# Gate products ahead of the convolution's layer norm, and five of 31 convolution taps summed on GpSimd

## The chip, the cores and the metric

The kernel runs on one core of one Trainium2 chip. The time is device microseconds (us) of one execution; a verdict compares runs of two kernels on the same chip. One execution is also recorded by the hardware profiler, and the trace comes from that one. Engines are named as the profile does: PE (TensorE matmuls), DVE (VectorE), ACT (ScalarE), POOL (GpSimd), SP (SyncE, which issues most weight transfers).

## The reference, cut to what matters

Three transformer blocks run over one sequence of 512 tokens of 1,024 channels, in float32. The change lies in the first. That block normalises its input and projects it to queries, keys and values of a sparse attention, to the two inputs of a convolution branch, and to two sets of gates. Attention and convolution branch are each multiplied by a gate, added, projected, and added to the input; a feed-forward part follows. The convolution branch is

```python
def conformer_conv(u_a, u_b, conv_w, conv_b, ln_g, ln_b, w_o, b_o):
    z = u_a * jax.nn.sigmoid(u_b)
    zp = jnp.pad(z, ((0, 0), (CONV_WIDTH - 1, 0), (0, 0)))      # 31 taps
    z = lax.conv_general_dilated(zp, conv_w, ...,
                                 feature_group_count=CONV_DIM) + conv_b
    mu = jnp.mean(z, axis=-1, keepdims=True)
    var = jnp.mean(jnp.square(z - mu), axis=-1, keepdims=True)
    zn = (z - mu) * lax.rsqrt(var + EPS) * ln_g + ln_b
    return jax.nn.silu(zn) @ w_o + b_o
```

It is a depthwise convolution: each channel has its own 31 weights, and each output is the sum of 31 shifted and scaled copies of `z`. Its output is normalised over the channels, so the mean needs all 1,024 of them. The gate of the branch is a product of the block's normalised input with a 1,024 x 1,024 matrix; it doesn't depend on the convolution.

## The kernel before

Activations lie with channels on the 128 partitions and the 512 tokens along them, so 1,024 channels are eight chunks, and the stack `X[:, c]` holds one chunk each. A float32 product is made of three matmuls of fp32r halves: `gemm` (L168 to L173) takes, for each of eight input chunks, `wh` by the high part, `wh` by the low part and `wl` by the high part, 24 matmuls of 128x512 for one output chunk. A weight unit of 512 KB (`wunit`) is fetched by an SP transfer into one of two `wst` buffers, ACT copies it in two pieces to `wh` (L155), POOL subtracts to get the remainder `wl` (L156), with four buffers of each kind. So every unit of weights needs SP, ACT and POOL before PE can use it, and PE has to be done before the buffers come free.

Block 1 runs in stages. In the projections, gates and inputs of the convolution are made chunk by chunk: `conv_gate` and `conv_in` (L650 to L664) leave a padded `z` of one chunk, and `conv_taps` (L666) sums its taps into a PSUM tile `y`: ACT writes the first tap with the bias (L671), DVE adds thirty (L673), ACT copies the sum to `X[:, c]` (L674). Between them come the keys, values and queries: rotary products on POOL (L706), stacks of split keys and queries (`stacks`, L1690; POOL at L1698 and L1705), and the compressed keys (L754 to L756). Attention then runs over four groups and four blocks of queries: scores, row maximum on DVE (L937), exponential on ACT, scaling by 1/sum partly on POOL (L949), transposes and products (L956 to L967). Three of the eight chunks of the convolution and the attention gates are interleaved with it.

After attention (L1006 on) the branch's layer norm collects its sums with `norm.feed(k)`: a first column sum of chunks 0 and 1 (L292, a matmul with ones into `pm` at L198, ACT at L295) gives a rough mean `c`, each chunk is centred by it (L306) and its square summed (L277), and two more column sums give mean and variance (L321 to L326); Ln and Exp on ACT (L216, L217) and three DVE operations (to L224) give `r`. Then eight gate products `w1_gc` run, DVE scales each by the block's norm (L680) and ACT takes the tanh (L1015). Last, each chunk is scaled by `r` (L336), passed through the activation (L1024), split into `zn` (L193, L194) and multiplied by `w1_co`; L1031 and L1032 multiply by the gate and add attention.

The order on each engine is fixed when the program is built: a scheduler goes through the program as written and by priorities. Weight units have a raised priority. The convolution's taps have one lowered by 3,000, so that they are put where DVE has nothing more urgent; wherever they land, each engine executes its own list strictly in order.

Of the kernel before, what the change touches and what calls it, by code (L numbers as in the profile page):

```python
# [13 lines left out]
AF = mybir.ActivationFunctionType  # L14
# [3 lines left out]
ADD, SUB, MUL, MAX, MIN = ALU.add, ALU.subtract, ALU.mult, ALU.max, ALU.min  # L18

P = 128  # L20
T = 512
NT = 8
# [16 lines left out]
MTB = 1  # L39
PS2 = dict(g=2, m=2, iv=2, rc=1, o=1)  # L40
HP = (30,60,0)
FIN = ("DDDDDDDD", "DDPDDPDD")
FLO = 1000
SQP = (2,4)
# [546 lines left out]
def block1(K, X, entry):  # L591

    K.hp = HP[0]
    nc, I, tc = K.nc, K.I, K.tc
# [23 lines left out]
    for k in range(NT):  # L618
# [4 lines left out]
        s = acc[k] if k < 2 else K.tmp()  # L623
# [33 lines left out]
    def conv_in(c):  # L657
        pa = K.gemm(K.gps(), gx, K.wunit(I["w1_ua"][c]))
        a = K.tmp()
        nc.vector.scalar_tensor_tensor(a, pa, 0.5, R, op0=MUL, op1=MUL)  # L660
        z = pz.tile([P, 30 + T], F32, tag="z", name=K.nm("z"))
        nc.gpsimd.memset(z[:, :30], 0.0)
        nc.vector.scalar_tensor_tensor(z[:, 30:], zb.pop(c), 1.0, a, op0=ADD, op1=MUL)
        conv_taps(c, z)  # L664

    def conv_taps(c, z):  # L666
        w = lambda k: K.v("conv_w", c * 31 + k)
        with tc.high_priority(offset=-LOW):

            y = K.ps("y")  # L670
            nc.scalar.activation(y, z[:, 0:T], AF.Identity, scale=w(0), bias=K.v("conv_b", c))  # L671
            for k in range(30, 0, -1):
                nc.vector.scalar_tensor_tensor(y, z[:, k:k + T], w(k), y, op0=MUL, op1=ADD)  # L673
            nc.scalar.activation(X[:, c], y, AF.Copy)  # L674

    def proj(w, scale=None, out=None):
        ps = K.gemm(K.gps(), gx, w if isinstance(w, list) else K.wunit(w))
        s = K.tmp() if out is None else out
        if scale is None:
            nc.vector.tensor_tensor(s, ps, R, MUL)  # L680
        else:
            nc.vector.scalar_tensor_tensor(s, ps, scale, R, op0=MUL, op1=MUL)
        return s

    sw = []
    for i in range(2):
        t = pA.tile([P, T], F32, name=f"swp{i}")
# [141 lines left out]
    for i in range(2):  # L829
        t = pA.tile([P, 640], F32R, name=f"KCz{i}")  # L830
# [4 lines left out]
    for i in range(2):  # L835
        t = pA.tile([P, 2, 4, P], F32R, name=f"PCz{i}")
# [170 lines left out]
    sC = ExitStack()  # L1007
    norm = Norm(0, K, X, 1e-6, sC)
    pC = sC.enter_context(tc.tile_pool(name="b1d", reuse_waits="tile", bufs=16))
    for k in range(NT):  # L1010
        norm.feed(k)
    sgc = []
    for m in range(NT):
        sgc.append(pC.tile([P, T], F32, tag="gc", bufs=8, name=K.nm("gc")))
        nc.scalar.activation(sgc[m], proj(I["w1_gc"][m]), AF.Tanh, scale=0.5)  # L1015
    zn = []
    alloc = lambda tag: (lambda: pC.tile([P, T], F32R, tag=tag, name=K.nm(tag)))
    for k in range(NT):
        norm.apply(k)
        y = X[:, k]  # L1020
        nc.scalar.activation(y, y, AF.Identity, scale=K.v("conv_norm_g", k), bias=K.v("conv_norm_b", k))
        t = norm.tmp()
# [31 lines left out]
    for qi, nk in enumerate(FFN_CUTS):  # L1054
        hid = []
        for m in range(at, at + nk):
# [3 lines left out]
            t = K.tmp()  # L1060
# [11 lines left out]
        for m in range(NT):  # L1072
            ps = K.gemm(K.gps(), hid, down(m))
            if tail:
                y = K.tmp()
# [86 lines left out]
def block2(K, X, entry, es):  # L1162
    K.hp = HP[1]
    nc, I, tc = K.nc, K.I, K.tc
# [544 lines left out]
def block3(K, X, rms, out, norm, es):  # L1709
    K.hp = HP[2]  # L1710
    nc, I, tc = K.nc, K.I, K.tc
# [305 lines left out]
    def after(m, sl):  # L2017
# [4 lines left out]
        with tc.high_priority(offset=0 if sl.stop == T else -FLO):  # L2022
            for k in range(NT):
                x = X[:, k, sl]
                if FIN[sl.stop == T][k] == "D":
                    nc.vector.scalar_tensor_tensor(x, x, K.v("g_final", k), r6.R[:, sl], op0=MUL, op1=MUL)
# [8 lines left out]
def program(tc, I, out, first=1, last=3):  # L2035
    with ExitStack() as es:
# [7 lines left out]
        if first == 1:  # L2044
            block1(K, X, entry)
        else:
            tc.nc.sync.dma_start(X, I["x_in"].rearrange("(c p) t -> p c t", p=P))
            K.psum(g=5, m=3)
# [36 lines left out]
```

## Time and profile before

| | us |
|---|---|
| median of 3 runs | 2908.86 |
| lowest and highest | 2906.74, 2912.71 |
| the profiled execution | 2904.16 |
| its span in the trace | 2902.4 |
| TensorE's mean granted clock in it | 0.972 of full speed |

In the profile an engine's busy time leaves out its waits and its register and semaphore instructions. A wait is put down to what released it last. In the timeline a row with x4 stands for four instructions that followed without a gap, and the bracket gives the idle time in front of it and its releaser. "PEclk" is the granted clock, with 1.00 for 2.4 GHz and 0.50 for 1.2.

### The profile page before, as it was taken

To read this page: it belongs to the slowest core of one execution; us is meant where nothing else is said; L and a number is where in the kernel's file an instruction comes from. 1 tells how busy PE (TensorE), PEld (TensorE's weight loads), DVE (VectorE), ACT (ScalarE), POOL (GpSimd) and SP (SyncE) were. 2 spreads that over 40 slices of the span, in tenths; PEclk is the share of its full clock that TensorE was granted. 3 is DMA by queue.
4 is the path that set the end of the run, shared out by engine and by line. 5 is a ranking of instruction groups with operands and counts; after the bars stand their busy time and mean duration, and the time that the engine had idled before them with its cause. 6 is when DMAs were issued, how large, how long until landed. Compare 5 with 4: busy or idle time off the path is not lost.

```text
span 2902.4 us, 34153 instructions
## 1 busy us (share of the span) xinstructions
PE 2676.3 (92%) x12206; PEld 2120.0 (73%) x12206; DVE 1780.9 (61%) x2825; ACT 1283.2 (44%) x2317; POOL 1306.6 (45%) x1023
## 2 busy tenths in 40 slices
PE   7899999699999988988889999999988889999997
PEld 5677776478888856766676788877766678788885
DVE  7889899965243596776774821126877765422246
ACT  4357875533222354444443533332556652322234
POOL 6554432554444454333332644454544344444443
PEclk9999999799999999999999999999999899999999
DMA  3321111232322222222222222232222122222223
GB/s 115 114 86 54 54 38 37 77 105 91 98 95 94 95 67 96 70 78 73 70 70 68 67 101 95 95 116 88 94 89 75 49 80 87 92 98 95 95 95 102
DMA packets 79193, 243.32 MB, mean 84 GB/s; under 512 B 11312, under 2 KB 15320, under 8 KB 79024
## 3 DMA queue, kind: packets, MB, share of 16 engines
q1 hardware_dynamic: 79024, 241.15, 25.3%
q8 instruction: 96, 1.57, 0.2%
q14 instruction: 73, 0.60, 0.1%
HBM read 230.96 MB, written 4.52 MB: 81 GB/s over the span
## 4 chain that ended last, share of the span: by engine, by line
PE 63%; DVE 23%; ACT 6%; DMA 3%; issue 3%; POOL 2%; SPq 0%; DVEq 0%; ACTq 0%; POOLq 0%
PE pg L172 18%; PE pg L173 18%; PE pg L171 18%; DMA B<-diag 2%; DVE p L1894 1%; DVE py L673 1%; DVE X L336 1%; DVE QK L1310 1%; PE ppt L956 1%; POOL wl L156 1%; DMA diag<-dg 1%; DVE ln L277 1%; DVE Zt L1416 1%; PE ps L934 1%; DVE Z L1417 1%
## 5 line engine op out<-in xcount | busy, mean ns | idle before, releaser
L156 POOL TENSOR_TENSOR wl<-wst,wh 128x512 fp32r<-128x512 f32 (+1 forms) x808 | 1099.9, 1367 | 1367.1 <-ACT wh L155 1285.7
L155 ACT ACTIVATE wh<-wst 128x512 fp32r<-128x512 f32 (+1 forms) x808 | 500.8, 627 | 1102.1 <-PE pg L172 918.1
L171 PE MATMUL pg<-op,wh 128*128 128x512 f32 (+1 forms) x2008 | 812.7, 405 | 38.9 <-ACT wh L155 19.5
L172 PE MATMUL pg<-op,wh 128*128 128x512 f32 (+1 forms) x2008 | 808.6, 403 | 2.6 <-DVE op L191 2.4
L173 PE MATMUL pg<-op,wl 128*128 128x512 f32 (+1 forms) x2008 | 807.2, 402 | 3.9 <-POOL wl L156 3.9
L171 PEld LDWEIGHTS pg<-op,wh 128*128 128x128 f32 (+1 forms) x2008 | 386.7, 193 | 120.9 <-ACT wh L155 20.1
L173 PEld LDWEIGHTS pg<-op,wl 128*128 128x128 f32 (+1 forms) x2008 | 386.2, 192 | 83.6 <-POOL wl L156 6.7
L172 PEld LDWEIGHTS pg<-op,wh 128*128 128x128 f32 (+1 forms) x2008 | 387.3, 193 | 82.2 <-DVE op L191 5.8
L171 PE MATMUL pg<-hid,wh 128*128 128x512 f32 x688 | 272.2, 396 | 0.9 <-DVE hid L190 0.9
L173 PE MATMUL pg<-hid,wl 128*128 128x512 f32 x688 | 272.1, 396 | 0.0
L172 PE MATMUL pg<-hid,wh 128*128 128x512 f32 x688 | 271.8, 395 | 0.2 <-DVE hid L191 0.2
L673 DVE SCALAR_TENSOR_TENSOR py<-z,vec,py 128x512 f32<-128x512 f32 x240 | 180.2, 751 | 10.9 <-ACT py L671 6.2
L1120 DVE TENSOR_TENSOR X<-X,pg 128x512 f32<-128x512 f32 x56 | 38.5, 688 | 222.1 <-PE pg L173 222.1
L171 PEld LDWEIGHTS pg<-hid,wh 128*128 128x128 f32 x688 | 129.2, 188 | 32.9 <-DVE hid L190 1.3
L172 PEld LDWEIGHTS pg<-hid,wh 128*128 128x128 f32 x688 | 129.2, 188 | 31.9 <-DVE hid L191 0.5
L173 PEld LDWEIGHTS pg<-hid,wl 128*128 128x128 f32 x688 | 129.2, 188 | 31.3 <-issue 0.2
L190 DVE CAST hid<-t 128x512 fp32r<-128x512 f32 x86 | 53.0, 616 | 145.7 <-ACT t L1097 145.0
L1111 DVE SCALAR_TENSOR_TENSOR t<-pg,R 128x512 f32<-128x512 f32 x32 | 22.1, 691 | 84.0 <-PE pg L173 83.9
L938 ACT ACTIVATE P<-ps,s 128x128 f32<-128x128 f32 (+3 forms) x128 | 66.4, 523 | 11.6 <-DVE s L937 9.5
L191 DVE TENSOR_TENSOR hid<-t,hid 128x512 fp32r<-128x512 f32 x86 | 63.6, 740 | 3.0
L937 DVE TENSOR_REDUCE s<-ps 128x1 f32<-128x128 f32 (+3 forms) x128 | 60.1, 483 | 8.1 <-PE ps L936 6.6
L960 DVE TENSOR_TENSOR PTl<-ppt,PTh 128x512 fp32r<-128x512 f32 x80 | 53.4, 684 | 4.7 <-ACT PTh L959 3.9
(523 smaller groups left out, 4344.3 us busy)
## 6 DMA issues: line engine op xcount, KB each, us to landing
wst<-in_w_f_dram SPq DMA_DIRECT2D x64, 512.0 KB
wst<-in_w_up_dram SPq DMA_DIRECT2D x32, 512.0 KB
wst<-in_w_down_dram SPq DMA_DIRECT2D x32, 512.0 KB
wst<-in_w_ga_dram SPq DMA_DIRECT2D x24, 512.0 KB
wst<-in_w_fg_dram SPq DMA_DIRECT2D x22, 512.0 KB
wst<-in_w_fu_dram SPq DMA_DIRECT2D x22, 512.0 KB
wst<-in_w_q_dram SPq DMA_DIRECT2D x16, 512.0 KB
wst<-in_w_out_dram SPq DMA_DIRECT2D x16, 512.0 KB
```

The source lines that it names most:

```text
L155: nc.scalar.activation(h, st, AF.Copy)
L156: nc.gpsimd.tensor_tensor(l, st, h, SUB)
L171: self.nc.tensor.matmul(ps, lhsT=wh, rhs=h[:, sl], start=first and k == 0, stop=False)
L172: self.nc.tensor.matmul(ps, lhsT=wh, rhs=l[:, sl], start=False, stop=False)
L173: self.nc.tensor.matmul(ps, lhsT=wl, rhs=h[:, sl], start=False, stop=last and k == n - 1)
L190: nc.vector.tensor_copy(h, src)
L191: nc.vector.tensor_tensor(l, src, h, SUB)
L673: nc.vector.scalar_tensor_tensor(y, z[:, k:k + T], w(k), y, op0=MUL, op1=ADD)
L937: nc.vector.tensor_reduce(mx[:, h:h + 1], S[:, :L], AX, MAX, negate=True)
L938: nc.scalar.activation(Pt[h][:, :L], S[:, :L], AF.Exp, bias=mx[:, h:h + 1], accum_out=den[:, h:h + 1])
L960: nc.vector.tensor_tensor(tl, pt, th, SUB)
L1120: nc.vector.tensor_tensor(X[:, m], X[:, m], ps, ADD)
```

## The change

Two things change in block 1. In `conv_taps`, POOL computes the first tap with the bias into `X[:, c]`, then four times a product into a temporary tile and a sum into `X[:, c]`. DVE's first operation adds tap 5 to that sum and writes `y`; 25 taps follow instead of thirty. ACT's first tap goes; its copy to `X[:, c]` stays. POOL so has nine operations more a chunk, 72 in all; DVE four fewer a chunk, 32 in all. The other part moves the loop of the eight gate products ahead of the loop of `norm.feed`.

```diff
+GTAPS = 5
...
         with tc.high_priority(offset=-LOW):
 
+            s = X[:, c]
+            nc.gpsimd.tensor_scalar(s, z[:, 0:T], w(0), K.v("conv_b", c), op0=MUL, op1=ADD)
+            for k in range(1, GTAPS):
+                t = K.tmp()
+                nc.gpsimd.tensor_scalar(t, z[:, k:k + T], w(k), None, op0=MUL)
+                nc.gpsimd.tensor_tensor(s, s, t, ADD)
             y = K.ps("y")
-            nc.scalar.activation(y, z[:, 0:T], AF.Identity, scale=w(0), bias=K.v("conv_b", c))
-            for k in range(30, 0, -1):
+            nc.vector.scalar_tensor_tensor(y, z[:, GTAPS:GTAPS + T], w(GTAPS), s, op0=MUL, op1=ADD)
+            for k in range(30, GTAPS, -1):
                 nc.vector.scalar_tensor_tensor(y, z[:, k:k + T], w(k), y, op0=MUL, op1=ADD)
             nc.scalar.activation(X[:, c], y, AF.Copy)
...
-    for k in range(NT):
-        norm.feed(k)
+
     sgc = []
     for m in range(NT):
         sgc.append(pC.tile([P, T], F32, tag="gc", bufs=8, name=K.nm("gc")))
         nc.scalar.activation(sgc[m], proj(I["w1_gc"][m]), AF.Tanh, scale=0.5)
+    for k in range(NT):
+        norm.feed(k)
```

In the changed kernel the new lines are L672 (first tap), L675 and L676 (products and sums on POOL), L678 (DVE's first), L680 (DVE's taps) and L681 (ACT's copy); lines after them stand 7 or 8 higher than before, and helpers at the top one higher (L156 is L157).

POOL's order in the projection stage, before: after a rotary product (L706) come only weight remainders (`wl`), two to a unit.

```order
45 L706 TENSOR_TENSOR t_432<-swp_295,ropes 128x512
46 L156 TENSOR_TENSOR wl_646<-wst_643,wh_645 128x512
47 L156 TENSOR_TENSOR wl_650<-wst_643,wh_649 128x512
48 L156 TENSOR_TENSOR wl_668<-wst_665,wh_667 128x512
49 L156 TENSOR_TENSOR wl_672<-wst_665,wh_671 128x512
```

The same place in the changed kernel, where `z_473` is the convolution's chunk 0:

```order
45 L713 TENSOR_TENSOR t_432<-swp_295,ropes 128x512
46 L672 TENSOR_SCALAR X<-z_473,vec 128x512
47 L157 TENSOR_TENSOR wl_662<-wst_659,wh_661 128x512
48 L675 TENSOR_SCALAR t_477<-z_473,vec 128x512
49 L675 TENSOR_SCALAR t_480<-z_473,vec 128x512
50 L676 TENSOR_TENSOR X<-X,t_477 128x512
51 L675 TENSOR_SCALAR t_483<-z_473,vec 128x512
52 L676 TENSOR_TENSOR X<-X,t_480 128x512
53 L157 TENSOR_TENSOR wl_666<-wst_659,wh_665 128x512
54 L676 TENSOR_TENSOR X<-X,t_483 128x512
55 L675 TENSOR_SCALAR t_486<-z_473,vec 128x512
56 L676 TENSOR_TENSOR X<-X,t_486 128x512
```

The chunk's nine operations now stand around the two remainders of the next unit; each of the chunks 0 to 4 has such a place ahead of POOL's first scaling of attention, the other three within attention.

DVE's order at the end of attention (`attn` is attention's output, L960 and L967 its last split), before: the taps of chunk 7, `py_4552`, all stand behind it, and ahead of the norm's L296.

```order
624 L673 SCALAR_TENSOR_TENSOR py_3670<-z_3667,vec,py_3670 128x512 x2
625 L998 TENSOR_TENSOR attn<-po_4995,lo_5125 64x2x128 x2
626 L292 TENSOR_TENSOR ln_5222<-X 128x512
627 L878 SCALAR_TENSOR_TENSOR attn<-t_5164,attn 128x512
628 L878 SCALAR_TENSOR_TENSOR attn<-t_5203,attn 128x512
629 L673 SCALAR_TENSOR_TENSOR py_3670<-z_3667,vec,py_3670 128x512 x4
630 L673 SCALAR_TENSOR_TENSOR py_4552<-z_4549,vec,py_4552 128x512 x30
631 L296 SCALAR_TENSOR_TENSOR ln_5222<-c_5226,ln_5222 128x512
```

The same place now, with the eight gate products' scaling at L687 behind it:

```order
625 L680 SCALAR_TENSOR_TENSOR py_4621<-z_4605,vec,py_4621 128x512
626 L293 TENSOR_TENSOR ln_5598<-X 128x512
627 L1005 TENSOR_TENSOR attn<-po_5059,lo_5189 64x2x128 x2
628 L680 SCALAR_TENSOR_TENSOR py_4621<-z_4605,vec,py_4621 128x512
629 L885 SCALAR_TENSOR_TENSOR attn<-t_5228,attn 128x512
630 L885 SCALAR_TENSOR_TENSOR attn<-t_5267,attn 128x512
631 L687 TENSOR_TENSOR t_5322<-pg_5287,R_43_242 128x512
...
638 L687 TENSOR_TENSOR t_5595<-pg_5560,R_43_242 128x512
639 L297 SCALAR_TENSOR_TENSOR ln_5598<-c_5602,ln_5598 128x512
```

Over the whole of block 1, DVE had 83 taps ahead of attention's first row maximum, 121 within attention and 36 behind its last split; it now has 92, 114 and 2.

PE's order behind attention, before: a column sum (`pm`) stands ahead of the gate products (`pg`).

```order
2347 L967 MATMUL po_4995<-PCz_1199,VC 128x512
2348 L198 MATMUL pm_5224<-ln_5222,ones 128x512
2349 L171 MATMUL pg_5294<-op_140,wh_5297 128x512
```

Now all 192 gate matmuls, 2349 to 2540, follow attention directly, and the three column sums and the first output products follow them:

```order
2540 L174 MATMUL pg_5560<-op_227,wl_5568 128x512
2541 L199 MATMUL pm_5600<-ln_5598,ones 128x512
2542 L199 MATMUL pm_5642<-ln_5598,ones 128x512
2543 L199 MATMUL pm_5644<-ln_5606,ones 128x512
2544 L172 MATMUL pg_5741<-zn_5674,wh_5744 128x512
```

The two later column sums stood within the third gate unit before.

## Rows read from the trace of the kernel before

**Rows 1.** The page, part 1: busy time, share of the span and instructions of each engine.

```profile
PE 2676.3 (92%) x12206; PEld 2120.0 (73%) x12206; DVE 1780.9 (61%) x2825; ACT 1283.2 (44%) x2317; POOL 1306.6 (45%) x1023
```

**Rows 2.** Windows: us; busy us of PE, PEld, DVE, ACT, POOL; PE clock, DMA share, GB/s.

```profile
71.00:161.00 90.00, 80.00 (x394) 63.19 (x393) 78.87 (x104) 34.27 (x60) 51.65 (x42) 1.00 0.35 117
...
180.00:487.00 307.00, 296.82 (x1603) 227.31 (x1601) 278.04 (x551) 238.19 (x586) 125.29 (x113) 1.00 0.16 52
...
504.00:523.00 19.00, 0.33 (x2) 0.00 (x0) 17.21 (x25) 2.83 (x6) 0.00 (x0) 0.63 0.00 0
```

**Rows 3.** Waits, 71 to 161 us: who waited for whom; us, times, longest.

```profile
POOL wl L156 <- ACT wh L155: 39.5, 20, 7.8
ACT wh L155 <- PE pg L172: 22.2, 13, 2.9
...
PE pg L755 <- POOL wl L156: 4.0, 8, 1.0
```

**Rows 4.** Timeline of PE, 486 to 588 us: start, us, instruction, idle before.

```profile
486.49 0.62 PE L967 MATMUL po<-PCz,VC 128*128 128x512 f32 x2
...
523.06 0.79 PE L171 MATMUL pg<-op,wh 128*128 128x512 f32 x1 [18.74 <-ACT wh L155]
...
534.88 3.78 PE L198 MATMUL pm<-ln,ones 128*128 128x512 f32 x4 [6.71 <-DVE ln L277]
...
541.15 0.39 PE L171 MATMUL pg<-op,wh 128*128 128x512 f32 x1
...
564.37 0.39 PE L171 MATMUL pg<-op,wh 128*128 128x512 f32 x1
...
573.89 0.40 PE L171 MATMUL pg<-zn,wh 128*128 128x512 f32 x1
...
587.05 0.39 PE L172 MATMUL pg<-zn,wh 128*128 128x512 f32 x1
```

**Rows 5.** Timeline of DVE, 495 to 580 us.

```profile
495.07 23.71 DVE L673 SCALAR_TENSOR_TENSOR py<-z,vec,py 128x512 f32<-128x512 f32 x30 [1.48 <-ACT py L671]
...
519.93 0.69 DVE L296 SCALAR_TENSOR_TENSOR ln<-c,ln 128x512 f32<-128x512 f32 x1 [1.15 <-ACT c L295]
...
523.55 1.76 DVE L277 TENSOR_TENSOR ln<-ln,X 128x512 f32<-128x512 f32 x1
...
534.75 0.68 DVE L277 TENSOR_TENSOR ln<-ln,ln 128x512 f32<-128x512 f32 x1
...
548.68 0.69 DVE L224 SCALAR_TENSOR_TENSOR r<-ln,r 128x512 f32<-128x512 f32 x1
...
549.89 8.02 DVE L336 TENSOR_TENSOR X<-X,r 128x512 f32<-128x512 f32 x6
...
577.52 1.67 DVE L194 SCALAR_TENSOR_TENSOR zn<-X,zn 128x512 fp32r<-128x512 f32 x1
```

**Rows 6.** Lines L673, L663, L937: ns min/median/max, first and last start.

```profile
L673 DVE SCALAR_TENSOR_TENSOR py<-z,vec,py x240: 718/756/757, 77.4 to 518.0; 128x512 f32<-128x512 f32 x120
...
L663 DVE SCALAR_TENSOR_TENSOR z<-zb,t x8: 671/1221/1804, 70.8 to 425.5; 128x512 f32<-128x512 f32 x8
...
L937 DVE TENSOR_REDUCE s<-ps x128: 229/476/692, 175.5 to 468.4; 128x1 f32<-128x128 f32 x32, 128x1 f32<-128x256 f32 x32, 128x1 f32<-128x384 f32 x32, 128x1 f32<-128x512 f32 x32
```

**Rows 7.** POOL's groups by form over the span: busy us, mean ns, idle before.

```profile
L706 POOL TENSOR_TENSOR t<-swp,ropes 128x512 f32<-128x512 f32 x14 | 18.5, 1323 | 6.9 <-DMA swp<-t 6.8
...
L949 POOL TENSOR_TENSOR P<-P,s 128x512 f32<-128x512 f32 x8 | 8.6, 1097 | 2.7 <-DVE s L941 2.6
...
L688 POOL MEMSET swp<- 128x512 f32 x2 | 1.0, 524 | 0.0
```

**Rows 8.** ACT's groups, 536 to 550 us.

```profile
L1015 ACT ACT_TABLE_LOAD x1 | 1.3, 1283 | 0.0
L216 ACT ACT_TABLE_LOAD x1 | 1.3, 1283 | 1.2 <-DVE ln L326 1.2
L217 ACT ACT_TABLE_LOAD x1 | 1.3, 1283 | 0.0
```

## The prediction

> **What bounds the kernel now.** I first read the page's busy shares: PE is busy for 92% of the span and every other engine for at most 61% [rows 1], so the kernel as a whole is bound by PE, and an edit is worth only what it changes in PE's idle or slow time, or in a stage where another engine holds PE back. I then read the engines' busy time in the six stretches of block 1 that the change touches [rows 2].
>
> - Projections (71 to 161 us): PE busy 80.00 of 90 us, DVE 78.87, POOL 51.65. No engine is free. The waits of this stretch [rows 3] show what joins them: POOL's weight remainders wait for ACT's copies 20 times, 39.5 us in all, ACT waits for PE to free weight buffers (22.2 us), PE waits for POOL's remainders 8 times. That is one ring, DMA, ACT, POOL, PE and back, of two stages and four half-unit buffers. POOL's idle 38 us are waits inside the ring, not spare time that is all usable.
> - Attention (180 to 487 us): PE 296.82 of 307 us, DVE 278.04, POOL 125.29. At most 10 us can be won here, and POOL has room.
> - Gates and norm (487 to 587 us): the one place where PE stands idle for long. PE has 0.33 us of work in the 19 us from 504 to 523, while DVE has 17.21.
>
> The PE timeline there [rows 4] says why: attention ends at 487.1 (486.49 + 0.62), the first column sum and two gate units follow, then PE waits 18.74 us for ACT's `wh`. ACT stands behind its copy of chunk 7's convolution, which needs DVE's 30 taps, 23.71 us from 495.07 [rows 5]. Later PE waits 6.71 us for the norm's sums.
>
> **Part A, the taps: what goes.** DVE loses 4 taps and ACT its seed in each of 8 chunks: 32 taps at a median 756 ns [rows 6], 24 us of DVE. In the order, all of chunk 7 stood behind attention before; now only two taps do. So the 23.7 us wait in the gate stretch is gone: the remaining taps fit between attention's work. Attention itself holds 114 taps instead of 121, 5 us less of DVE.
>
> **Part A: what comes.** POOL gets 40 products of one tensor by a column scalar, and 32 sums of two tensors. The sums have a row: 1,323 ns for the same shape at L706 [rows 7]. The products have none. Below, the nearest row is a 128x512 memset, 524 ns; above, L949, a product by a broadcast operand, 1,097 ns. A product reads one tensor and writes one, nearer to the memset than to a two-operand form; I take 0.75 us and keep both ends. Sum: 40 x 0.75 + 32 x 1.32 = 72 us of POOL (63 to 86).
>
> 45 of the 72 (25 products, 20 sums, chunks 0 to 4) stand in POOL's queue ahead of attention's first P scaling, beside the same 111 other operations: 25 x 0.75 + 20 x 1.32 = 45 us (40 to 54) into a stretch where POOL had 38 us idle. That alone overflows by 7 us (2 to 16). The rest comes from where they stand. In POOL's order chunk 0's nine now straddle both remainders of the next weight unit; in before nine remainders stood in a row there. A remainder behind nine operations comes about 9 us late; the ring holds two units ahead, 2 x 5.45 us of PE work (24 matmuls at 0.227 us, from the starts 541.15 and 564.37, 102 matmuls apart [rows 4]), so part of each delay is absorbed, part reaches PE, and PE's 10 us of idle give some back. Walking the units with these durations, each of chunks 1 to 4 leaves 10 to 13 us of delay, falling to about 7 before the next, and the key stacks, also POOL's and now behind chunk 4's nine, are late by 13. I take **+13 us** until attention starts (+5 if the buffers take most of it, +25 if products cost 1.10 and nothing is won back).
>
> The Trainium skill (GPSIMD Engine Reference, section 3.1) says the same against this part: elementwise work stays on DVE, since GpSimd takes about twice as long on a two-input operation. The trace agrees on the sums, 1,323 ns [rows 7] against 756 ns for a whole tap on DVE [rows 6]. That page's 1.03 cycles an element at 1.2 GHz for a one-input body would make a product about 0.44 us plus dispatch, an estimate; the sum by it would be near the lower end, POOL's 45 operations then costing 37 us.
>
> **Attention.** 5 us less of DVE work where DVE is 91% busy. Against it: the seed `y = z*w5 + s` now stands in DVE's order behind `z` by 13 other rows at chunk 6 and 7 at chunk 7, about 6 and 4 us, while POOL's nine operations need 9 to 12: DVE, and behind it the row maxima that PE and ACT wait for, stand 5 to 8 us at each. POOL running more also lengthens DVE operations that read two SBUF tensors: `z`, one such, took 671 to 1,804 ns, the taps, which read PSUM beside `z`, 718 to 757 [rows 6]. Since attention's idle PE time is 10 us and taps fill gaps, I take **+2 us** (-5 to +8).
>
> **Part B, gates first.** Gates cost the same; they move. PE's order after attention is now 8 x 24 gate matmuls, then the norm's column sums, then the output products. Nothing holds these 192: 192 x 0.227 = 43.6 us. Only then may the norm's first column sum run, though DVE has had its input since attention ended. The chain from there:
> - first column sum, ACT's copy, L296: 2.3 us (before, 1.15 from the last tap's end to L296, for the copy, and L296's 0.69 [rows 5]; the rest is the matmul);
> - centring and sums: 15.5 us before (519.93 to 535.43), 1.1 us lost on each of two rows at 1.76 instead of 0.68 [rows 5]: 14;
> - column sums to `r`: 14 us before (535.4 to 549.4), less three of ACT's five table loads there at 1.28 us [rows 8], which go as the tanhs no longer mix in; I take 11.8, since PE's column sums now find a PE that has stood idle, and ACT's other two stay;
> - `zn`: before 549.89 to 579.2, with six L336 at 8.02 us (1.34 each instead of 0.68) and gate evictions between. Without them 8 x (0.60 + 0.60 + 0.34 + 0.60) = 17.5;
> - the output products follow `zn` chunk by chunk; units 0, 1 and eight matmuls are done 2.5 us later.
>
> 43.6 + 2.3 + 14 + 11.8 + 17.5 + 2.5 = 91.7 us. Before, the 56th output matmul starts at 587.05 [rows 4], 100 us after attention. So **-8 us** (-14 to -2): of 25 us of PE waits removed (18.74 + 6.71), most returns as one idle stretch of 33 us behind them, where nothing is left to put beside the norm. Rows from block 1's output on are the same.
>
> **Sum.** +13 + 2 - 8 = +7 us on the profiled run's 2904.2 us, 2911. That run lies 4.7 us under the median of the three runs, 2908.9; on the median's scale I forecast 2916.
>
> **Rivals.**
> 1. *The ring absorbs POOL's work* (chance 0.24). Products at the memset's 0.52 us make 39.5 us, just the idle 38; bursts hide in the weight buffers: +3 - 4 - 8 = -9, 2900. For it: PE waited for POOL only 4.0 us in 8 waits [rows 3]. Against: those idle waits are spread in 20 pieces of 2 us on average, a burst is 9 to 12.
> 2. *The full gate gain* (0.10), the other side further out: DVE's wait goes, PE's order lets the norm run early, POOL hidden: -25, 2884. Against: the column sums stand behind all 192 gate matmuls in PE's order.
> 3. *POOL's burst becomes DVE's wait* (0.22): products near 1.10 us, and DVE's seeds of chunks 0, 6, 7 stop everything behind them, key stacks late by 20 and more: +25 + 8 - 4 = +29, 2938. It decides from about 0.95 us a product. The Trainium skill (SBUF — State Buffer, section SBUF: two separate sides) has DVE operations with two SBUF inputs and GpSimd lock each other out; `z` at up to 1,804 ns fits.
> 4. *The terms cancel* (0.14): +8 + 0 - 8, 2909.
> 5. The forecast (0.30): +7, of its own 2911 to 2922.
>
> **Chances and range.** A measurement here tells about 0.2%, 5.8 us, from no change. Faster by more: rivals 1 (most of it) and 2, with a little of 4: 0.34. Within: rival 4, the lower edge of the forecast and the upper of rival 1: 0.22. Slower: rival 3 and most of the forecast: 0.44. Both signs hold much, so the likeliest case's own range stands above. The range for all: from -21 (most of rival 2 left out) to +31, the upper ends of projection and attention with the gate gain at its low bound: 2888 to 2940.
>
> **What would show it.** In the changed profile: L672 and L675 near 0.75 us, L676 near 1.3; waits of PE, DVE or ACT on POOL in 71 to 185 us grown by about 10 us, the first row maximum (L937, 175.5 before [rows 6]) 13 us later; no 18.7 us wait of PE behind attention, 192 gate matmuls at one pace, then one idle stretch of about 33 us at a lowered clock. The forecast is wrong if attention starts within 5 us of before (rival 1), if products are over 0.95 us (rival 3), or if the distance from attention's end to the 56th output product is under 85 us or over 98.

## The result, and the profile after

The changed kernel takes 2962.74 us at the median (4 runs, 2956.54 to 2966.64) against 2910.78 for the kernel before on the same chip (4 runs): 1.0179 of it, 95% interval 1.0163 to 1.0194. It is 52 us slower, where 2916 was forecast with a range up to 2940.

Three points split the span: the first row maximum of attention (line L937 before, L944 now), attention's last matmul, and the last output product of the convolution branch (the last of 192 on `zn`). All rows of the following table are read at those points; "attention" is the distance between the first and the second (to the end of the matmul, its start + 0.39), "stretch" between the second and the third, "behind" the rest of the span. The rows e1 to e14 are the experiments; each ratio is to runs of the kernel before on the same chip. The medians of the kernel before lie between 2906.92 and 2913.87 us on the chips used, so kernels of different chips are compared by these ratios and by the stages, and not by their medians.

| kernel | attention starts | attention | stretch | behind | median us | ratio to before, 95% interval |
|---|---|---|---|---|---|---|
| before | 175.5 | 311.6 | 131.7 | 2283.6 | | |
| the change | 216.8 | 330.5 | 123.1 | 2291.0 | 2962.74 | 1.0179 (1.0163 to 1.0194) |
| e1 two-operation product | 197.7 | 323.5 | 123.4 | 2285.3 | 2933.53 | 1.0083 (1.0062 to 1.0104) |
| e2 gates only | 176.2 | 311.7 | 148.5 | 2287.4 | 2926.24 | 1.0062 (1.0043 to 1.0081) |
| e3 taps only | 213.3 | 332.2 | 107.9 | 2287.2 | 2941.98 | 1.0112 (1.0092 to 1.0132) |
| e4 forms | 214.5 | 325.4 | 123.4 | 2287.8 | 2952.88 (one run) | |
| e5 direct write, gates first | 178.1 | 304.0 | 143.4 | 2284.7 | 2913.53 | 1.0012 (1.0002 to 1.0023) |
| e6 direct write, five gates first | 177.8 | 304.4 | 134.9 | 2285.5 | 2904.03 | 0.9985 (0.9975 to 0.9996) |
| e7 sum joined last, gates first | 196.4 | 308.3 | 123.4 | 2283.2 | 2917.76 | 1.0028 (1.0018 to 1.0037) |
| e8 five taps, late chunks | 176.8 | 311.2 | 119.0 | 2290.0 | 2898.76 | 0.9961 (0.9948 to 0.9975) |
| e9 direct write only | 176.7 | 304.2 | 133.1 | 2284.0 | 2906.60 | 0.9978 (0.9968 to 0.9988) |
| e10 nine taps, late chunks | 177.8 | 321.3 | 111.9 | 2291.1 | 2903.96 | 0.9972 (0.9963 to 0.9981) |
| e11 eleven taps, late chunks | 179.2 | 333.1 | 104.0 | 2289.2 | 2906.92 | 0.9980 (0.9970 to 0.9991) |
| e12 sum joined last, gates behind | 195.6 | 308.3 | 109.1 | 2290.2 | 2902.31 | 0.9964 (0.9953 to 0.9976) |
| e13 two taps early, five late | 179.4 | 313.4 | 111.5 | 2284.9 | 2897.90 | 0.9965 (0.9952 to 0.9979) |
| e14 five taps late, joined last | 176.4 | 308.6 | 117.4 | 2284.3 | 2891.18 | 0.9942 (0.9930 to 0.9955) |

For the change: +41.3 in the projections, +18.9 in attention, -8.6 in the stretch, +7.4 behind, 59.0 us of span. Nothing behind the stretch is changed, and that part lies between 2283.2 and 2291.1 in the sixteen profiles with no order that follows the edits, so the 7.4 is not put down to the change. The other three terms add up to 51.6 us.

The page's busy shares, part 1 of the changed kernel's page, for [rows 1]:

```profile
PE 2692.4 (91%) x12206; PEld 2134.2 (72%) x12206; DVE 1752.5 (59%) x2793; ACT 1277.6 (43%) x2306; POOL 1393.6 (47%) x1095
```

POOL has 87 us more, DVE 28 less. The same engines by stretch of the changed kernel (columns as in [rows 2]): the projections' window, and 20 us behind the gates.

```profile
71.00:161.00 90.00, 64.10 (x285) 49.78 (x284) 59.85 (x77) 22.54 (x39) 78.79 (x60) 0.85 0.24 80
600.00:620.00 20.00, 3.75 (x4) 1.17 (x4) 18.24 (x25) 8.12 (x12) 6.45 (x4) 0.59 0.00 0
```

In the projections POOL is now busy for 78.79 of 90 us, and PE does 64.10 us of work instead of 80.00. Behind the gates PE has 3.75 us of work in 20, at a granted clock of 0.59, near the lower level (0.50, 1.2 GHz).

The same columns from 71 us to the start of attention and for attention, first of the kernel before, then of the changed one:

```profile
71.00:175.50 104.50, 91.08 (x453) 72.72 (x452) 91.97 (x125) 38.34 (x67) 62.17 (x50) 0.98 0.34 112
175.50:487.10 311.60, 301.42 (x1641) 231.81 (x1639) 282.34 (x561) 240.15 (x592) 127.88 (x115) 1.00 0.16 51
...
71.00:216.80 145.80, 103.75 (x445) 81.89 (x444) 100.55 (x134) 36.58 (x64) 126.07 (x97) 0.84 0.25 80
216.80:547.30 330.50, 306.70 (x1647) 235.74 (x1647) 277.58 (x554) 238.37 (x588) 162.11 (x141) 0.97 0.15 47
```

Of the 41.3 us in the projections, 28.6 are more idle time of PE and 12.7 are longer busy time for about the same matmuls, at a granted clock of 0.84 instead of 0.98; in attention it is 13.6 and 5.3 of 18.9. The forecast priced every matmul ahead of attention's end at one pace.

The added lines (minimum, median and maximum in ns, first and last start), and the row maximum of [rows 6]:

```profile
L672 POOL TENSOR_SCALAR X<-z,vec x8: 762/766/1387, 71.3 to 480.8; 128x512 f32<-128x512 f32 x8
...
L675 POOL TENSOR_SCALAR t<-z,vec x32: 1552/1563/1878, 74.2 to 488.6; 128x512 f32<-128x512 f32 x32
...
L676 POOL TENSOR_TENSOR X<-X,t x32: 1253/1273/1309, 77.8 to 491.5; 128x512 f32<-128x512 f32 x32
...
L944 DVE TENSOR_REDUCE s<-ps x128: 259/484/693, 216.8 to 528.5; 128x1 f32<-128x128 f32 x32, 128x1 f32<-128x256 f32 x32, 128x1 f32<-128x384 f32 x32, 128x1 f32<-128x512 f32 x32
```

L672, which multiplies and adds, takes 766 ns, the sums 1,273. The 32 products at L675 take 1,563 ns, twice what the first tap takes for more arithmetic, and above both ends of the bound from [rows 7]. The waits of the projections, 71 to 161 us, of the changed kernel, where [rows 3] had 39.5 us of POOL waiting and 4.0 of PE:

```profile
PE pg L762 <- POOL wl L157: 11.1, 8, 3.9
...
DVE py L678 <- POOL X L676: 9.2, 1, 9.2
...
PE pg L174 <- POOL wl L157: 7.9, 2, 7.1
POOL wl L157 <- ACT wh L156: 7.6, 5, 2.8
```

The ring has turned round: POOL waits for ACT 7.6 us, PE waits for POOL's remainders 11.1 and 7.9, and DVE once 9.2 us for POOL's five taps. Later, at 204.92 us, PE waits 9.4 us for a rotary product of DVE (L715) that stands behind taps in DVE's order; for the same product it waited 3.4 us before. In attention DVE waits for POOL twice, 17.0 us in all (waits of 217 to 547 us), and PE then waits for DVE's work and for ACT's, which needs it, 9.39 and 8.35 us in PE's timeline:

```profile
DVE py L678 <- POOL X L676: 17.0, 2, 9.7
...
404.19 0.79 PE L970 MATMUL po<-PTl,VS 128*128 128x512 f32 x1 [9.39 <-DVE PTl L967]
...
497.72 0.69 PE L941 MATMUL ps<-sk,sk 128*128 128x384 f32 x1 [8.35 <-ACT P L945]
```

The second wait shows in DVE's timeline at chunk 7 (start, duration, instruction, idle before), where all of DVE stands from 485.47 on,

```profile
485.05 0.42 DVE L944 TENSOR_REDUCE s<-ps 128x1 f32<-128x256 f32 x1 [2.01 <-PE ps L943]
492.80 1.74 DVE L678 SCALAR_TENSOR_TENSOR py<-z,vec,X 128x512 f32<-128x512 f32 x1 [7.32 <-POOL X L676]
```

and POOL's timeline of these microseconds shows what it stands for: one chunk's nine operations, 12 us long, in one piece (the rows left out are products and sums too).

```profile
480.77 0.77 POOL L672 TENSOR_SCALAR X<-z,vec 128x512 f32<-128x512 f32 x1 [0.79 <-DVE z L664]
481.51 3.11 POOL L675 TENSOR_SCALAR t<-z,vec 128x512 f32<-128x512 f32 x2
...
490.17 2.59 POOL L676 TENSOR_TENSOR X<-X,t 128x512 f32<-128x512 f32 x2
492.72 1.26 POOL L157 TENSOR_TENSOR wl<-wst,wh 128x512 fp32r<-128x512 f32 x1
```

The stretch behind attention, on PE's timeline, answers to [rows 4]:

```profile
546.70 0.63 PE L974 MATMUL po<-PCz,VC 128*128 128x512 f32 x2
...
590.71 1.02 PE L199 MATMUL pm<-ln,ones 128*128 128x512 f32 x2
605.73 3.75 PE L199 MATMUL pm<-ln,ones 128*128 128x512 f32 x4 [14.00 <-DVE ln L278]
622.52 1.19 PE L172 MATMUL pg<-zn,wh 128*128 128x512 f32 x2 [13.04 <-ACT X L1029]
...
670.43 0.40 PE L174 MATMUL pg<-zn,wl 128*128 128x512 f32 x1
```

From 547.3 to 590.7 the gate products run at one pace, then PE waits 14.00 us for the centring and sums and 13.04 for `zn`. This is the forecast's "one idle stretch of 33 us": 31.8 us from 590.71 to 622.52, of which 27.0 are waits.

### The profile page after: what moved, and what is told of

Its sections match the earlier page's. It is cut to its first block, busy times and chain, and to the rows that moved or that the text cites. A ratio compares the mean times of both kernels' runs of the same rounds, so it can differ in the third digit from the quotient of the medians.

```text
span 2961.4 us, 34193 instructions
## 1 busy us (share of the span) xinstructions
PE 2692.4 (91%) x12206; PEld 2134.2 (72%) x12206; DVE 1752.5 (59%) x2793; ACT 1277.6 (43%) x2306; POOL 1393.6 (47%) x1095
## 4 chain that ended last, share of the span: by engine, by line
PE 58%; DVE 18%; ACT 4%; DMA 3%; issue 2%; POOL 1%; SPq 0%; DVEq 0%; ACTq 0%; POOLq 0%
PE pg L173 17%; PE pg L172 17%; PE pg L174 17%; DMA B<-diag 2%; DVE p L1902 1%; DVE QK L1318 1%; DVE X L337 1%; DMA diag<-dg 1%; DVE ln L278 1%; DVE Zt L1424 1%; PE ppt L963 0%; DVE vT L1318 0%; DVE Z L1425 0%; ACT wh L156 0%; PE piv L1445 0%
## 5 line engine op out<-in xcount | busy, mean ns | idle before, releaser
L157 POOL TENSOR_TENSOR wl<-wst,wh 128x512 fp32r<-128x512 f32 (+1 forms) x808 | 1091.2, 1356 | 1317.2 <-ACT wh L156 1239.2
L156 ACT ACTIVATE wh<-wst 128x512 fp32r<-128x512 f32 (+1 forms) x808 | 501.2, 627 | 1165.9 <-PE pg L173 943.8
L172 PE MATMUL pg<-op,wh 128*128 128x512 f32 (+1 forms) x2008 | 813.9, 406 | 17.5 <-DVE zb L654 5.5
L680 DVE SCALAR_TENSOR_TENSOR py<-z,vec,py 128x512 f32<-128x512 f32 x200 | 150.1, 751 | 3.7
L945 ACT ACTIVATE P<-ps,s 128x128 f32<-128x128 f32 (+3 forms) x128 | 66.3, 521 | 16.0 <-DVE s L944 13.6
L944 DVE TENSOR_REDUCE s<-ps 128x1 f32<-128x128 f32 (+3 forms) x128 | 60.6, 485 | 13.3 <-PE ps L943 11.4
L941 PE MATMUL ps<-sk,sk 128*128 128x256 f32 (+2 forms) x128 | 48.1, 376 | 9.7 <-ACT P L945 8.8
```

What stands on the lines that cost most here:

```text
L156: nc.scalar.activation(h, st, AF.Copy)
L157: nc.gpsimd.tensor_tensor(l, st, h, SUB)
L172: self.nc.tensor.matmul(ps, lhsT=wh, rhs=h[:, sl], start=first and k == 0, stop=False)
L941: nc.tensor.matmul(S[:, :N], lhsT=ql, rhs=kh[:, :N], start=True, stop=False)
L944: nc.vector.tensor_reduce(mx[:, h:h + 1], S[:, :L], AX, MAX, negate=True)
L945: nc.scalar.activation(Pt[h][:, :L], S[:, :L], AF.Exp, bias=mx[:, h:h + 1], accum_out=den[:, h:h + 1])
```

## The experiments

**e1, the product's price.**

```diff
-                nc.gpsimd.tensor_scalar(t, z[:, k:k + T], w(k), None, op0=MUL)
+                nc.gpsimd.tensor_scalar(t, z[:, k:k + T], w(k), 0.0, op0=MUL, op1=ADD)
```

> The change with one edit: POOL's products get a second operation, add 0.0, so that they have the form of the first tap (multiply, add), which took 766 ns at the median in the changed kernel while the products with one operation took 1,563. Theory 1, the price of the product is what the forecast mis-sized: the product falls to about 0.77 us, a chunk's nine operations from 12.1 to about 9 us, 16 us of POOL work go from ahead of attention; attention starts at 188 to 200 us instead of 216.8, lasts some 318 instead of 331, and the time is 2918 to 2935. Rival, the place of the nine operations in POOL's fixed order costs most, whatever they take: attention still starts after 205 and the time is over 2945. Second rival, the product costs 1.56 with two operations too: no change against the changed kernel, 2963.

The products' line and the first row maximum of this kernel:

```profile
L675 POOL TENSOR_SCALAR t<-z,vec x32: 682/692/1133, 73.7 to 462.8; 128x512 f32<-128x512 f32 x32
...
L944 DVE TENSOR_REDUCE s<-ps x128: 258/483/693, 197.7 to 502.3; 128x1 f32<-128x128 f32 x32, 128x1 f32<-128x256 f32 x32, 128x1 f32<-128x384 f32 x32, 128x1 f32<-128x512 f32 x32
```

692 ns instead of 1,563 from one added operation that does nothing. Attention starts 19.1 us earlier, and DVE's wait for POOL within attention falls from 17.0 us (9.7 and 7.3) to 9.4 (the waits of 198 to 521 us).:

```profile
DVE py L678 <- POOL X L676: 9.4, 2, 5.5
```

Attention lasts 323.5 us, 7.0 less than in the change, where some 318 were expected. The time is 1.0083 of before instead of 1.0179, some 28 us less; the two terms in the profiles are 26. So about half of the 52 us were the product's price. The other 24 to 26 are there with products as cheap as the forecast had assumed.

**e2, the gates alone.** The loop of the gate products ahead of `norm.feed`, the convolution as before.

> The gate products ahead of the norm, and the convolution as before. By the forecast's gate term, which the changed kernel bore out (93 us from attention's end to the 56th output product, against 100 before), PE runs five gate units beside DVE's 36 last taps, the scaling of the gates follows them, and the stretch is 92 to 96: -5 to -8 us, 2903 to 2906. Rival: the taps stand ahead of all eight scalings on DVE, PE runs out of result buffers and the stretch is 100 or more: 2911 or slower. Second rival: the early gates are worth the whole idle time of PE, 25 us: 2886.

The rival's numbers, slower than before by some 18 us (1.0062), but not its mechanism of result buffers. PE's timeline shows a wait longer than the 18.74 us that the gates were to cover:

```profile
520.73 0.79 PE L171 MATMUL pg<-op,wh 128*128 128x512 f32 x1 [21.98 <-ACT wh L155]
```

and ACT's timeline shows that the weight copy (L155) is ready to run only behind ACT's copy of chunk 7 (L674), for which ACT has stood 23.78 us:

```profile
519.56 0.60 ACT L674 ACTIVATE X<-py 128x512 f32<-128x512 f32 x1 [23.78 <-DVE py L673]
520.05 1.14 ACT L155 ACTIVATE wh<-wst 128x512 fp32r<-128x512 f32 x2
```

PE runs two units and waits for DVE's taps after all; the norm then starts behind all the gates. To the 56th output product it is 117 us, to the last one 148.5, 16.8 more than before.

**e3, the taps alone.** The change with `norm.feed` back ahead of the gate products.

> The five taps on POOL as in the change, and the gate products behind the norm's first sum as before. Attention starts at 217 us and lasts 331 as in the change. Theory: the parts stand in each other's way. With no taps left at attention's end the norm can run beside the gates, and the stretch from attention's end to the 56th output product is 70 to 80 us, against 93 with the gates first: the time is 2940 to 2952, faster than both parts together. Rival, the parts add up: without the gate part's 7 us the time is 2968 to 2972.

2941.98, some 20 us faster than both parts together (1.0112 against 1.0179), and 76 us to the 56th output product, as expected; to the last one, which the table and the later runs use, the stretch is 107.9 us. Taking the taps out of attention's end is worth 23.8 us (131.7 to 107.9); putting the gates first gives 15.2 of them back.

**e4, forms of a product on POOL.** The product of taps 1 to 4 is written differently by chunk; chunks 3 and 7 leave the taps' weights out, so this kernel is for the prices alone.

```diff
-                nc.gpsimd.tensor_scalar(t, z[:, k:k + T], w(k), None, op0=MUL)
+                if c in (0, 4):    nc.gpsimd.tensor_scalar(t, z[:, k:k + T], w(k), None, op0=MUL)
+                elif c in (1, 5):  nc.gpsimd.tensor_scalar(t, z[:, k:k + T], w(k), 0.0, op0=MUL, op1=ADD)
+                elif c in (2, 6):  nc.gpsimd.tensor_tensor(t, z[:, k:k + T], w(k).to_broadcast([P, T]), MUL)
+                elif c == 3:       nc.gpsimd.tensor_scalar(t, z[:, k:k + T], 0.5, None, op0=MUL)
+                else:              nc.gpsimd.tensor_scalar(t, z[:, k:k + T], 0.5, 0.0, op0=MUL, op1=ADD)
```

> One look at what forms of a product cost on POOL, 128x512 in float32, by chunk of the convolution: chunks 0 and 4 one operation with a column operand (as in the change), 1 and 5 multiply by the column and add the constant 0.0, 2 and 6 a product of two tensors of which one is the column broadcast, 3 one operation with the constant 0.5, 7 multiply by 0.5 and add 0.0. The products of chunks 3 and 7 so leave the tap's weight out. Theory 1, one operation is the slow form: 1.56 us in chunks 0, 3 and 4, 0.77 in 1, 5 and 7, the broadcast 1.1 to 1.3. Rival, the column operand is slow unless there are two: 1.56 in chunks 0, 1, 4 and 5, 0.77 or less in 3 and 7. Second rival, writing to a temporary tile is slow, whatever the form: 1.56 in all.

In the order of the branches above, one row each:

```profile
L676 POOL TENSOR_SCALAR t<-z,vec x8: 1555/1566/1863, 74.3 to 198.8; 128x512 f32<-128x512 f32 x8
...
L678 POOL TENSOR_SCALAR t<-z,vec x8: 682/686/693, 94.1 to 294.1; 128x512 f32<-128x512 f32 x8
...
L680 POOL TENSOR_TENSOR t<-z,vec x8: 1029/1036/1491, 122.2 to 392.5; 128x512 f32<-128x512 f32 x8
...
L682 POOL TENSOR_SCALAR t<-z x4: 1482/1495/1498, 156.3 to 164.7; 128x512 f32<-128x512 f32 x4
...
L684 POOL TENSOR_SCALAR t<-z x4: 617/620/624, 477.3 to 481.6; 128x512 f32<-128x512 f32 x4
```

Theory 1: one operation takes 1,566 ns with a column and 1,495 with a constant, two take 686 and 620. The column costs some 70 ns, the missing second operation some 880. The broadcast product, 1,036, lies between; the forecast's upper bound had come from such a form.

**e5, gates first without ACT's copy.** As e2, and

```diff
-                nc.vector.scalar_tensor_tensor(y, z[:, k:k + T], w(k), y, op0=MUL, op1=ADD)
-            nc.scalar.activation(X[:, c], y, AF.Copy)
+                nc.vector.scalar_tensor_tensor(X[:, c] if k == 1 else y, z[:, k:k + T], w(k), y, op0=MUL, op1=ADD)
```

> No taps on POOL, all eight gates first, and one more edit: DVE's last tap of a chunk writes X itself, so ACT's copy of the sum goes. Theory: with the gates first alone PE waited 22 us behind its second unit because ACT's copy of chunk 7, which needs DVE's last taps, stood in ACT's queue ahead of the next weight copy. Without that copy the stretch from attention's end to the last output product falls from 148.5 us to 121 to 126 (the norm's chain behind 43.6 us of gates, as in the changed kernel, 123.1), the time is 2897 to 2903. Rival: the scalings of the gates stand behind the same taps on DVE, PE runs out of result buffers, and the stretch stays over 135: 2912 or slower.

The stretch is 143.4, not 121 to 126. The rival's number, though not by its mechanism: PE does not run out of result buffers, it waits 16.79 us for a weight copy again, and ACT's timeline has another instruction in front of it, the tanh of the first gate (L1012), which waits for DVE's scaling (L679) behind the same taps:

```profile
490.31 1.14 ACT L155 ACTIVATE wh<-wst 128x512 fp32r<-128x512 f32 x2
514.75 0.63 ACT L1012 ACTIVATE gc<-t 128x512 f32<-128x512 f32 x1 [23.30 <-DVE t L679]
515.29 1.13 ACT L155 ACTIVATE wh<-wst 128x512 fp32r<-128x512 f32 x2
```

The norm's sums wait behind all the gates, on PE's timeline:

```profile
515.95 0.79 PE L171 MATMUL pg<-op,wh 128*128 128x512 f32 x1 [16.79 <-ACT wh L155]
...
560.72 3.75 PE L198 MATMUL pm<-ln,ones 128*128 128x512 f32 x4 [14.13 <-DVE ln L277]
```

**e6, five gates first.** As e5, with `norm.feed` between the fifth and the sixth gate.

> As the run before, but five gates ahead of the norm's first sum and three behind it. Theory: five units, 27 us, cover DVE's last taps, and the other three run beside the norm's centring and sums, which in the changed kernel ran beside nothing; the stretch is 110 to 117 us against 131.7 before and 123.1 in the change: 2888 to 2895. Rival: gates beside the norm slow it (their scalings and tanhs, with two more table loads, stand in the chain), the stretch is 122 or more, no better than with all eight first.

PE's timeline:

```profile
515.97 0.79 PE L171 MATMUL pg<-op,wh 128*128 128x512 f32 x1 [16.79 <-ACT wh L155]
...
548.74 3.75 PE L198 MATMUL pm<-ln,ones 128*128 128x512 f32 x4 [4.58 <-DVE ln L277]
```

The same 16.79 us wait, so five units do not cover the taps either. The norm's sums now wait 4.58 us instead of 14.13 in e5, since three gates run beside them, and the stretch falls from 143.4 to 134.9. That is in the range of the rival, but by the first wait, which the theory took for covered, and not by gates that slow the norm.

**e7, POOL's sum joined last.** The cut is against e1's kernel; the bias goes from POOL's first tap to ACT's.

```diff
-            nc.vector.scalar_tensor_tensor(y, z[:, GTAPS:GTAPS + T], w(GTAPS), s, op0=MUL, op1=ADD)
+            nc.scalar.activation(y, z[:, g:g + T], AF.Identity, scale=w(g), bias=K.v("conv_b", c))
...
-            nc.scalar.activation(X[:, c], y, AF.Copy)
+                nc.vector.tensor_tensor(s, y, s, ADD)
```

> The change with the two-operation product (2933.5), but POOL's sum joins at the end: ACT starts y with tap 5 and the bias, DVE adds taps 30 to 6, and a last DVE sum of y and POOL's part writes X; ACT's copy goes, POOL's work stays in its place. Theory, POOL's burst holds back the weight remainders: attention still starts at 194 to 200 us (197.7), it only lasts 312 to 317 instead of 323.5 since DVE waits no more in it: 2921 to 2928. Rival, DVE's wait for POOL at the start of a chunk is what costs in the projections: attention starts at 178 to 186: 2903 to 2914.

Attention starts at 196.4 us, about as with the seed on DVE (197.7), and lasts 308.3 instead of 323.5, less than the 312 to 317 expected; e9 shows below that the direct write alone is worth some 7 us of it. So in the projections DVE's wait for POOL is not what costs, at least with these products; POOL is busy for 79.56 of 90 us and PE for 73.83 (window of 71 to 161 us, and its waits):

```profile
71.00:161.00 90.00, 73.83 (x334) 57.43 (x333) 70.12 (x93) 28.45 (x49) 79.56 (x71) 0.89 0.26 91
```

```profile
PE pg L768 <- POOL wl L158: 6.0, 5, 2.8
...
PE pg L175 <- POOL wl L158: 4.6, 2, 3.9
```

**e8, late chunks only.** POOL sums five taps, two-operation form, in chunks 5 to 7; the gates stand behind.

> POOL sums five taps, with the two-operation product, only in chunks 5, 6 and 7, whose inputs come within attention; the gates stand where they stood before. Theory: without POOL's bursts in the projections attention starts at 175 to 177 us as before, lasts 312 to 320, and of DVE's last taps 20 stay behind attention instead of 36, so the stretch falls by 9 to 12 us: 2896 to 2906. Rival: DVE's wait for POOL at chunks 6 and 7 costs attention 12 us, as with all chunks, and takes the gain away: 2908 to 2914.

2898.76, 0.9961 of before. Attention starts at 176.8: without POOL's bursts in the projections there is no delay. On PE's timeline the wait of 18.74 us [rows 4] has become 7.68, with 22 taps behind attention's last split instead of 36:

```profile
511.42 0.79 PE L173 MATMUL pg<-op,wh 128*128 128x512 f32 x1 [7.68 <-ACT wh L157]
```

**e9, the direct write only.** The edit of e5, the gates where they stood.

> The kernel before with one edit: DVE's last tap of a chunk writes X, ACT's copy goes. No taps on POOL, the gates where they stood. It tells how much of the two runs with that edit came from it: theory, ACT no more waits in attention for DVE's last taps, attention lasts 304 us instead of 311.6 as in those runs, and the stretch after it grows by as much since the taps that remain are the same work for DVE: 2904 to 2910. Rival: the stretch stays at 131.7, and the edit alone is worth 5 to 8 us: 2900 to 2904.

2906.60, 0.9978 of before on its chip, some 6 us: the rival by its gain and its stretch, though the time itself lies in the theory's range, since before is 2913.87 on this chip. Attention lasts 304.2 us instead of 311.6 and the stretch hardly grows (133.1). What in attention ACT's copies had held up was not followed further.

**e10 and e11, nine and eleven taps in the late chunks.** The late chunks of e8 with the join of e7, with more taps; the other chunks are written as in e9, here and in e14.

> POOL sums nine taps of chunks 5, 6 and 7, joined at the end by a DVE sum that writes X, two-operation products, the gates where they stood, last taps of the other chunks written to X directly. Theory: no burst in the projections (start 175 to 179), no wait of DVE for POOL (attention 303 to 309), and 13 taps and a sum left behind attention instead of 36 taps, so that the stretch is 113 to 118: 2884 to 2892. Rival: POOL's work in attention, 50 us more, holds back the gates' weights there, attention is 315 or longer: 2896 or slower.

> As the run before with eleven taps of each of the three chunks on POOL, which leaves three taps and a sum behind attention. Theory: the stretch comes to 107 to 111, as where no taps were left (107.9), attention is 303 to 310: 2878 to 2888. Rival: POOL's part of chunk 7, eleven products and ten sums, some 21 us, comes too late for the sum that joins it, and DVE waits behind attention: 2890 or slower.

The stretch came out somewhat shorter than expected (111.9 and 104.0), attention far longer: 321.3 and 333.1 us, which gives the rivals' times without their mechanisms. POOL's timeline of e11 shows a part of why: between chunk 6's first operation and the next scaling of P (L962), 22.8 us of taps and remainders stand,

```profile
355.36 0.69 POOL L679 TENSOR_SCALAR X<-z,vec 128x512 f32<-128x512 f32 x1 [0.65 <-DVE s L921]
...
375.55 2.59 POOL L681 TENSOR_TENSOR X<-X,t 128x512 f32<-128x512 f32 x2
378.11 1.18 POOL L962 TENSOR_TENSOR P<-P,s 128x256 f32<-128x256 f32 x2
```

and PE's transposes wait 11.22 us for that scaling (PE's timeline, then the waits of 179 to 493 us):

```profile
378.77 1.47 PE L969 MATMUL ppt<-ident,P 128*128 128x128 f32 x4 [11.22 <-POOL P L962]
...
PE ppt L969 <- POOL P L962: 12.4, 3, 11.2
```

At chunk 7 POOL's work is as long, but PE waits hardly more than 1 us for the scaling. In e10 the three waits come to 4.6 us. PE's idle time in attention is 21 us longer in e11 than in e9 and 9 us longer in e10, so about half is explained; the rest was not followed.

**e12, joined last, gates behind.** e7 with `norm.feed` ahead of the gates.

> Taps on POOL in all eight chunks with the sum joined at the end, as in the run of 2918, but the gates where they stood before. Theory, the stages add up: start 196 to 198 (POOL's bursts in the projections), attention 307 to 310, the stretch 106 to 109 as with the taps alone instead of 123: 2900 to 2905. Rival: the gates first were worth their 7 us here too, with POOL's time in order: 2918 or slower.

The stages add up: 195.6, 308.3, 109.1, and 2902.31 us (0.9964). The gates first cost 14.3 us of stretch here (123.4 in e7), as they cost 15.2 between e3 and the change.

**e13, two taps early, five late.** What still stood open was whether the sum of POOL's work delays the projections or each operation does.

> POOL sums two taps of chunks 0 to 4 and five of chunks 5 to 7, two-operation products, joined at the end by a DVE sum that writes X, the gates where they stood. Theory, a stock of about 22 us of POOL work is absorbed in the projections (the delays of 41 and 21 us lie on a line of 1.08 us for each us of POOL work, which comes to nothing at 23): start 175 to 179, attention 304 to 309, the stretch 113 to 118: 2893 to 2899 by a before of 2911. Rival, every operation ahead of a remainder costs its time: 13 us later, 187 to 190, and 2905 or slower.

```profile
71.00:161.00 90.00, 78.04 (x376) 62.02 (x375) 77.40 (x103) 31.39 (x55) 62.53 (x53) 0.96 0.31 105
```

Attention starts at 179.4, 3.9 us late for 13.3 us of POOL's taps, and POOL has room again (62.53 of 90). With 43.2 us of taps (5 x 0.77 + 20 x 0.69 + 20 x 1.28, e1) it was 22.2, with 60.6 (the change) 41.3. So 9 of 13, 21 of 43 and 19 of 61 us are absorbed: some 20 us at most, and from 43 to 61 us of taps each further microsecond of POOL costs about one. It is not a stock that is free until it is used up, since 4 of the first 13 us were paid. Rival and theory were 187 to 190 and 175 to 179, so what counts is mainly the sum. Attention is 313.4, longer than expected, and why was not found.

**e14, five late taps, joined last.**

> POOL sums five taps of chunks 5, 6 and 7 only, joined at the end, and all chunks are written to X by DVE; the gates where they stood. Theory: start 176 to 178, attention 304 to 309 (the 304 of the direct write alone, and POOL's short bursts), the stretch 117 to 120 as with the late chunks alone: 2891 to 2898 by a before of 2911. Rival, POOL's bursts hold back its scalings in attention as with nine taps, attention is 313 or longer: 2901 or slower.

2891.18, 0.9942 of before (0.9930 to 0.9955): 16 us faster than the kernel before, the best of the study. The direct write alone gave 0.9978 (e9). The projections are as before ([rows 2], window of 71 to 161 us):

```profile
71.00:161.00 90.00, 79.21 (x392) 62.46 (x391) 79.78 (x106) 32.53 (x57) 51.57 (x42) 1.00 0.35 116
```

and in attention PE waits 1.5 us for POOL (waits of 176 to 485 us), as long as in the kernel before:

```profile
PE ps L947 <- POOL sk L1711: 1.5, 2, 1.0
```

## Why the prediction was wrong

The sum was +13 + 2 - 8; measured are +41.3, +18.9, -8.6. From +7 to 51.6 us, the product's price makes 26.1 (e1 against the change), the ring 9.2 (22.2 in e1 for 13), the wait in attention 9.9 (11.9 in e1 for 2), and the gates -0.6.

**The product's price.** The step "A product reads one tensor and writes one, nearer to the memset than to a two-operand form; I take 0.75 us and keep both ends" failed, ends included: 1,563 ns against 0.52 to 1.10. Neither row was a scalar operation, and the one that the forecast needed was in no trace of the kernel before. L672 came out at the 0.75 assumed for all. e1 and e4 show the missing second operation to be the cause, 19.1 of the 41.3 us in the projections and 7.0 of the 18.9 in attention. The Trainium skill (GPSIMD Engine Reference, section 3.1) has a body of one or two operations bound by the ports alike, at 1.03 cycles an element: that would leave no such difference, and the runs show 1,566 against 686 ns. Its rule to leave elementwise work on DVE the runs bear out for the taps of the projections (e1, e7, e13) and not for those that come within attention: e14 is 0.9942 of before, and e9, the same without POOL's taps, 0.9978.

**The ring.** Even at 692 ns, with 43 us of taps for the forecast's 45, attention started 22.2 us late, not 13. The walk, "10 to 13 us of delay, falling to about 7 before the next", gave back too much between the chunks: by e1, e13 and the change some 20 us at most are absorbed and the rest is paid in full. It also had no term for PE's clock, which fell with PE's idle time (0.98 before, 0.88 in e1 and 0.84 in the change, from 71 us to attention). Rival 1, that the ring absorbs POOL's work, held for about half of the 43 us. That POOL's and DVE's operations lengthen each other is too small to be the cause: in the window of 71 to 161 us the remainders take 1,382 ns on average for 1,327 before, 1.5 us over 27 of them, and `z`, which was to be lengthened, takes 684 to 1,783 ns in the change for 671 to 1,804 before; DVE's seed (L678), which is new, takes 1,198 ns on average where a tap took 756, 3.5 us over its eight.

**Attention.** "+2" was the sum of a gain and a wait. The wait was in the text (5 to 8 us at each of chunks 6 and 7) and was netted against 5 us of DVE work. It measured 17.0 us in the change, and 9.4 in e1, where the product cost what was assumed; so its size was about right, and what failed is that DVE's freed time and PE's 10 us of idle time would hide it: attention is 11.9 us longer in e1. e7, which takes the wait away, shortens attention by 15.2 against e1; of this the direct write gives some 7 (e9), so the wait is worth about 8, and some 4 stay open. Rival 3 had this mechanism and the point from which it decides, 0.95 us a product, and its total is 23 us too low. In the projections, where it has its +25, DVE's wait was not the cause with the cheaper product (e7).

**The gates.** The term measured -8.6 against -8 (123.1 - 131.7), and to the 56th output product it is 91.5 us for the 91.7 worked out. Each step was met within 2.5 us, and the errors cancel, which is partly luck: 43.4 us of gates for 43.6, 12.6 of centring and sums for 14, 11.5 to `r` for 11.8, 19.8 of `zn` for 17.5 (whose own factors, 8 x 2.14, make 17.1). But the text put it under part B, "so -8 us", and e3 shows it to be two terms: -23.8 for the taps that left attention's end, +15.2 for the gates put first. Part B alone costs 16.8 (e2). The sentence that should have been drawn from the own working is there: the column sums stand behind all 192 gate products, "where nothing is left to put beside the norm"; the comparison with the norm first, and no taps left, was not made.

**The full gate gain** (rival 2) fell for the reason given against it: the column sums start at 590.71 us, behind all 192.

## What to carry to other kernels

An engine that feeds others in a fixed order is not idle because its busy share is 57%: in this kernel, work put there in bursts cost little up to what the buffers behind it took up, some 20 us, and then its full time. Before work is moved to hide a wait, ask for every engine what stands at the head of its queue during that wait; here ACT's copy, then ACT's tanh, then POOL's scaling took the place of the wait that was removed. And when two edits remove the same wait, cost each with the other already made.

## What the runs showed of the hardware that was not expected

On POOL a 128x512 float32 multiplication by a column as a single operation took 1,566 ns, and the same with an addition of 0.0 behind it 686; by a constant 1,495 and 620 (e4). A tensor by a broadcast column took 1,036 (e4), a sum of two tensors 1,273 (the change).
